# A second block's gates, scans and softplus rounds put in another order

## The chip, the core and the metric

The kernel runs on one core of a Trainium2 chip. The metric is the device time of one execution in microseconds. The kernel before has a median of 1109.62 us over three runs (1109.36 to 1110.53).

## What is computed

The reference runs two transformer blocks on a sequence of 256 tokens of width 1024, all in float32. The first block (an SSD branch and a latent attention, a cross attention, a mixture of 32 experts) is not touched. The second block begins with a mixer, and that is where the change lies:

```python
proj = rmsnorm(h, attn_pre_norm) @ w_in            # 4*512 + 3*512 columns
hq, hf, hi, hg, sq, sk, sv = split(proj)
# HGRN2 on hq, hf, hi: 4 heads of 128
q = silu(hq)
log_f = logaddexp(log(lb), log1p(-lb) + log_sigmoid(hf))
k = -expm1(log_f)                                  # = 1 - f
# o_t = S_t^T q_t, with S_t = diag(f_t) S_{t-1} + k_t v_t^T, v = hi
o_hg = rmsnorm(o, hg_out_norm) * silu(hg)
# stick-breaking attention on sq, sk, sv: 8 heads of 64
z = q k^T / sqrt(64)
a = where(causal, exp(log_sigmoid(z) + rem), 0)    # rem: sum of -softplus(z) over the keys between
o_sb = rmsnorm(a @ v, sb_out_norm)
h = h + rmsnorm(concat(o_hg, o_sb) @ w_out, attn_post_norm)
```

A gated feed forward layer and a gated embedding follow.

## The kernel before

Every large product is made of **units**. A unit is 512 KB of weights: one load on the SP queue into a `raw` buffer (four of them), a cast by ScalarE into `whi` (L237), a subtraction by VectorE into the rest `wlo` (L238), then three matmuls on TensorE for each block of 128 rows (L263 to L265: high by high, and the two mixed ones). Four pairs of whi and wlo exist, and up to three units are split ahead of their use. Units come in a fixed order.

What else an engine does is put between the units by a planner, `schedule`. It takes several streams of `Item`s; an item has a cost, dependencies and for each dependency a latency, which a table (`LATENCY`) can replace by a number for that pair of names ('x#<z#' is any x item behind any z item). It always takes the first stream whose next item is due, and emits the items in that order; each engine then runs its own instructions in the order of emission. `run` emits the units' casts and subtractions ahead of the item that first uses them.

The second block's mixer has five streams: `start` (norms, `prep`), `hg` (HGRN2), `sb` (stick-breaking attention), `nrm` and `main`, which holds the units of w_in, then of w_out. These are the steps that matter here:

- `hqf`: eight chunks of 128 columns of w_in, q's four first, then the gate's four. `ev_hq` empties each chunk's PSUM buffer with a multiplication by the row norm `fr` (L1906) and then applies Silu to q (L1908), or for the gate a Sigmoid (L1911), lb and ol (L1912), max and min (L1913), a second Sigmoid (L1914) and ol (L1915).
- `gates` (item hga): Ln of the gate in place (L1944) and four scans along time (L1947), which read a mask out of the table `c2`; `prep` loads that whole table on POOL's queue (L1876) and sets the two buffers of `ql` and of `kl` to zero with POOL (L1883).
- `level(m)` for m = 128, 64, 32, ... 1 (item lv): differences of the sums, in `E`, on POOL (L1966, L1967, L1975, L1982, L1983), VectorE's t01 and a part of E (L1981, L1984), Exp on ScalarE, and q·E and k·E on VectorE as `ql` (L1992) and `kl` (L1993). `smat(m, t)` (item sm) makes their products on TensorE (L2004) in a PSUM buffer `ch`, of which there are four, and VectorE merges them into `S` (L2010 for the diagonal, a masked copy L2014 for the levels from 64 down).
- `ho`, `hm` and `mt0` close HGRN2: products with v (L2049, L2050), the norm, the gate (hm, L2057), and transposes (L438) whose results are split by ScalarE (mxh, L443) and VectorE (mxl, L444).
- For each of four pairs of heads the stick-breaking stream has `sb_z` (items z: scores L2072 and L2073, a copy L2078, min(z,-z) L2080, Exp and Ln L2081 and L2082, then max and add L2083 and the causal mask L2085), `sb_x` (items x: running sums as matmuls L2095 to L2100, VectorE's addition L2101, Exp L2102) and `sb_pv` (items pv: L2116 to L2118, a copy to `so` by ScalarE L2119).
- `sb_o` (items so) norms the result: two squares with a sum on ScalarE (L410), a power on POOL (L417, L418), a multiplication on VectorE (`hy`, L2038). Then come the transposes mt4 and the units of w_out, the attention's half of whose rows stands first.

Of the kernel before, what the change touches and what calls it, by code (L numbers as in the profile page):

```python
# [112 lines left out]
class K:  # L113
# [260 lines left out]
    def gemm_fm(self, w, c0, nch, kt, xT, evac, name, deps=(), held=None, wide=None):  # L374

        items = []
        hiT, loT = xT
        for i in range(0, nch, 2):  # L380
# [1924 lines left out]
```

## Time and profile before

| | |
|---|---|
| median of three runs | 1109.62 us |
| the profiled execution | 1108.28 us |
| its span, first to last instruction | 1106.5 us |
| TensorE busy | 1049.0 us (95%) |
| VectorE busy | 647.0 us (58%) |
| ScalarE busy | 525.3 us (47%) |
| GpSimd (POOL) busy | 142.2 us (13%) |
| mean granted TensorE clock | 0.979 |

The busy share is a mean over the whole program. The second block's mixer takes some 110 us from about 735 us on, and the views below are of that stretch. The granted clock is the share of full speed that TensorE was given: 1.0 is 2.4 GHz, 0.5 is 1.2 GHz.

### The profile page before, as it was taken

To read this page: it belongs to the slowest core of one execution; us is meant where nothing else is said; L and a number is where in the kernel's file an instruction comes from. 1 tells how busy PE (TensorE), PEld (TensorE's weight loads), DVE (VectorE), ACT (ScalarE), POOL (GpSimd) and SP (SyncE) were. 2 spreads that over 40 slices of the span, in tenths; PEclk is the share of its full clock that TensorE was granted. 3 is DMA by queue.
4 is the path that set the end of the run, shared out by engine and by line. 5 is a ranking of instruction groups with operands and counts; after the bars stand their busy time and mean duration, and the time that the engine had idled before them with its cause. 6 is when DMAs were issued, how large, how long until landed. Compare 5 with 4: busy or idle time off the path is not lost. (4 is left out here: it accounts for less than half of the span.)

```text
span 1106.5 us, 18028 instructions
## 1 busy us (share of the span) xinstructions
PE 1049.0 (95%) x7081; PEld 878.1 (79%) x7081; DVE 647.0 (58%) x1114; ACT 525.3 (47%) x944; POOL 142.2 (13%) x187
## 2 busy tenths in 40 slices
PE   6999999999999899999999897997999999999998
PEld 6999889878887798987766563697888788888876
DVE  4887788766766654545211110278865676667545
...
GB/s 251 193 191 153 130 119 136 133 200 125 137 144 115 315 347 316 160 220 322 421 413 420 412 418 414 312 175 122 188 71 123 134 204 177 190 187 173 221 143 95
DMA packets 135033, 241.29 MB, mean 218 GB/s; under 512 B 6924, under 2 KB 88336, under 8 KB 127776
## 3 DMA queue, kind: packets, MB, share of 16 engines
...
q14 instruction: 32, 0.26, 0.1%
...
## 5 line engine op out<-in xcount | busy, mean ns | idle before, releaser
L238 DVE TENSOR_TENSOR wlo<-raw,whi 128x1024 fp32r<-128x1024 f32 (+1 forms) x240 | 291.5, 1234 | 129.4 <-ACT whi L237 128.5
L237 ACT CAST whi<-raw 128x1024 fp32r<-128x1024 f32 (+1 forms) x240 | 244.9, 1041 | 97.3 <-PE acc L265 51.0
L273 PE MATMUL acc<-ew,whi 128*128 128x512 f32 x352 | 120.5, 394 | 0.8 <-DVE ew L444 0.8
L263 PE MATMUL acc<-uh,whi 128*128 128x256 f32 x384 | 111.2, 290 | 0.0
L264 PE MATMUL acc<-ul,whi 128*128 128x256 f32 x384 | 108.6, 283 | 0.0
L265 PE MATMUL acc<-uh,wlo 128*128 128x256 f32 x384 | 108.5, 283 | 0.0
L276 PE MATMUL acc<-ew,wlo 128*128 128x256 f32 x352 | 92.0, 282 | 0.0
L263 PEld LDWEIGHTS acc<-uh,whi 128*128 128x128 f32 x384 | 73.5, 191 | 0.8 <-issue 0.3
L264 PEld LDWEIGHTS acc<-ul,whi 128*128 128x128 f32 x384 | 73.6, 192 | 0.2
L265 PEld LDWEIGHTS acc<-uh,wlo 128*128 128x128 f32 x384 | 73.5, 191 | 0.0
L273 PEld LDWEIGHTS acc<-ew,whi 128*128 128x128 f32 x352 | 63.1, 188 | 12.6 <-DVE ew L444 1.0
L276 PEld LDWEIGHTS acc<-ew,wlo 128*128 128x128 f32 x352 | 66.1, 188 | 3.8
L1578 PE MATMUL acc<-ew,xe 128*32 128x256 f32 x688 | 57.5, 398 | 7.2 <-DMA ew<-in_w_exp_up_dram 3.7
L1537 PEld LDWEIGHTS acc<-Gr,h 128*128 128x128 f32 x256 | 54.5, 299 | 10.8 <-issue 9.8
L263 PE MATMUL acc<-whi,uh 128*128 128x512 f32 (+1 forms) x160 | 63.0, 394 | 0.0
L264 PE MATMUL acc<-wlo,uh 128*128 128x512 f32 (+1 forms) x160 | 61.5, 384 | 0.6 <-DVE wlo L238 0.6
L265 PE MATMUL acc<-whi,ul 128*128 128x512 f32 (+1 forms) x160 | 61.2, 383 | 0.0
L1537 PE MATMUL acc<-Gr,h 128*128 128x128 f32 x256 | 54.6, 373 | 6.0 <-DVE Gr L1518 6.0
L1578 PEld LDWEIGHTS acc<-ew,xe 128*32 128x32 f32 x688 | 34.5, 114 | 24.9 <-issue 5.9
L265 PE MATMUL acc<-ew,wlo 128*128 128x256 f32 x176 | 50.3, 286 | 0.9 <-DVE wlo L238 0.9
L263 PE MATMUL acc<-ew,whi 128*128 128x256 f32 x176 | 50.4, 286 | 0.8 <-ACT whi L237 0.5
L264 PE MATMUL acc<-ew,whi 128*128 128x256 f32 x176 | 50.3, 286 | 0.2
...
## 6 DMA issues: line engine op xcount, KB each, us to landing
...
```

Source lines behind the costliest of these rows:

```text
L237: self.nc.scalar.copy(hi[:, :m], u.raw[:, :m])
L238: self.nc.vector.tensor_sub(lo[:, :m], u.raw[:, :m], hi[:, :m].bitcast(F32))
L263: mm(out, ah, bh, start=start, stop=False)
L264: mm(out, ah, bl, start=False, stop=False)
L265: mm(out, al, bh, start=False, stop=stop)
L273: mm(out, ah, bw, start=(k == 0), stop=(k == last))
L276: mm(out[:, :T], al, b.hi[:, k, :], start=False, stop=False)
L1537: nc.tensor.matmul(p[:, j * P:(j + 1) * P], x, st["Gr"][:, t, :], start=(part is None and t == 0), stop=(t == 1 and (part is None or j == 3)))
L1578: nc.tensor.matmul(a[j][CAP * i:CAP * i + CAP, :256], xe[:, k, i * CAP:i * CAP + CAP], w, start=(k == 0), stop=(k == 7))
```

## The change

- Two more units are split before the row norm `fr` is computed (`more` twice), and a Sigmoid of one column stands before fr's copy, so that its table is loaded there.
- The gate's four chunks are projected first (`first=4`). Their PSUM buffers are emptied, and Sigmoid, lb and ol, max and min and the second Sigmoid are made over two or four chunks at once, at the fourth chunk; q's Silu is one activation over four chunks, at the last.
- The reset mask has a load of its own, early (`resets`). The table c2 gets 1024 columns of zeros; ql and kl are set to zero by four loads of these columns on POOL's queue, and c2's own load leaves them out.
- The scans wait for the gate's chunks alone, with a latency that puts them behind two splits; Ln goes in two halves. `level` is cut into `expo` (POOL's and VectorE's part of E, emitted two levels ahead) and the rest.
- In the softplus rounds max, add and mask become an item of their own, `sb_e`, between z and x.

In the diff the table's line is cut to the entries that change.

```diff
-C2_M, C2_TGE, C2_RST = 0, 896, 1024
-NCONST2 = 1280
+C2_M, C2_TGE, C2_RST, C2_ZERO = 0, 896, 1024, 1280
+NCONST2 = 2304
...
-LATENCY = {
...
-'sm128<lv128': 1.9,
...
-'hga<hqf.#': 0,
...
-'sm64<lv64': 3.7,
...
+LATENCY = {
...
+'sm128<lv128': 11.5,
...
+'hga<hqf.#': 4.0, 'sm0<hqf.#': 5.5,
...
+'sm64<lv64': 14.0,
...
-def gemm_fm(self, w, c0, nch, kt, xT, evac, name, deps=(), held=None, wide=None):
+def gemm_fm(self, w, c0, nch, kt, xT, evac, name, deps=(), held=None, first=0, wide=None):
...
-            u = self.unit(w, k0, nk, c0 + i * P, 256)
+            u = self.unit(w, k0, nk, c0 + (i + first) % nch * P, 256)
...
+        s = self.sp.tile([P, 4], F32, tag="rstd", name=self.nm("rstd"), bufs=6)
+        nc.scalar.activation(s[:, 0:1], self.half, AF.Sigmoid)
...
-    A["start"] = [Item(hsq(0), name="hs"), Item(more), Item(trans(1), cost=0.9, name="zt", deps=[("hs", 2)]),
+    def resets():
+        A["rst"] = self.sp.tile([P, D], F32, tag="un", name=self.nm("un"), bufs=2)[:, :T]
+        nc.gpsimd.dma_start(A["rst"], I["consts2"][:, C2_RST:C2_RST + T])
+    A["start"] = [Item(resets), Item(hsq(0), name="hs"), Item(more), Item(trans(1), cost=0.9, name="zt", deps=[("hs", 2)]),
...
-                  Item(spread, cost=0.4, name="fr", deps=[("f1", 4)]),
+                  Item(more, deps=[("f1", 3.9)]), Item(more), Item(spread, cost=0.4, name="fr", deps=[("f1", 4)]),
...
-        st["c2"] = pt([P, NCONST2], "c2")
-        nc.gpsimd.dma_start(st["c2"], I["consts2"])
+        st["c2"] = pt([P, C2_ZERO], "c2")
+        nc.gpsimd.dma_start(st["c2"], I["consts2"][:, :C2_ZERO])
...
         for n in ("ql", "kl"):
...
-                nc.gpsimd.memset(st[n, i], 0.0)
+                nc.gpsimd.dma_start(st[n, i].rearrange("p h t -> p (h t)"), I["consts2"][:, C2_ZERO:])
...
     def ev_hq(c, a):
...
-        x = st["q" if c < 4 else "k"][:, c % 4, :]
+        x = st["k" if c < 4 else "q"][:, c % 4, :]
...
-        if c < 4:
-            nc.scalar.activation(x, x, AF.Silu)
-        else:
-            f, lb, ol = st["sig"][:, c - 4, :], self.A["lb"][:, c - 4:c - 3], self.A["ol"][:, c - 4:c - 3]
-            nc.scalar.activation(f, x, AF.Sigmoid)
-            V.tensor_scalar(f, f, ol, lb, op0=ALU.mult, op1=ALU.add)
-            V.tensor_scalar(f, f, 2.0 ** -60, 1.0, op0=ALU.max, op1=ALU.min)
-            nc.scalar.activation(x, x, AF.Sigmoid, scale=-1.0)
-            V.tensor_scalar(x, x, ol, None, op0=ALU.mult)
+        sg, k = st["sig"], st["k"]
+        if c in (1, 3):
+            nc.scalar.activation(sg[:, c - 1:c + 1], k[:, c - 1:c + 1], AF.Sigmoid)
+        if c == 3:
+            for i in range(4):
+                V.tensor_scalar(sg[:, i], sg[:, i], self.A["ol"][:, i:i + 1], self.A["lb"][:, i:i + 1],
+                                op0=ALU.mult, op1=ALU.add)
+                if i % 2:
+                    h = sg[:, i - 1:i + 1]
+                    V.tensor_scalar(h, h, 2.0 ** -60, 1.0, op0=ALU.max, op1=ALU.min)
+            nc.scalar.activation(k, k, AF.Sigmoid, scale=-1.0)
+            for i in range(4):
+                V.tensor_scalar(k[:, i], k[:, i], self.A["ol"][:, i:i + 1], None, op0=ALU.mult)
+        if c == 7:
+            nc.scalar.activation(st["q"], st["q"], AF.Silu)
...
     held = []
-    main = self.gemm_fm(w, 0, 8, 8, U, ev_hq, "hqf", {0: [("hs", 0)], 2: [("zt", 2.5)]}, held)
+    main = self.gemm_fm(w, 0, 8, 8, U, ev_hq, "hqf", {0: [("hs", 0)], 2: [("zt", 2.5)]}, held, first=4)
...
     def gates():
...
-        nc.scalar.activation(sg, sg, AF.Ln)
+        for h in (0, 2):
+            nc.scalar.activation(sg[:, h:h + 2], sg[:, h:h + 2], AF.Ln)
...
-            V.tensor_tensor_scan(b[:, h, :], st["c2"][:, C2_RST:C2_RST + T], sg[:, h, :], 0.0,
+            V.tensor_tensor_scan(b[:, h, :], self.A["rst"], sg[:, h, :], 0.0,
...
-    def level(m):
+    def expo(m):
...
         def fn():
...
-            i = LV.index(m) % 2
-            E = pt([P, 4, T], "E", bufs=2)
-            ql, kl = st["ql", i], st["kl", i]
+            E = st["E", m] = pt([P, 4, T], "E", bufs=2)
...
-                nc.scalar.activation(E, E, AF.Exp)
...
-                v = lambda x: x.rearrange("p h (n s m) -> p h n s m", s=2, m=m)
...
                 if m == 64:
...
-                    nc.scalar.activation(ev[:, :, 0:4:2, :], ev[:, :, 0:4:2, :], AF.Exp)
-                    nc.scalar.activation(ev[:, :, 1:4:2, :], bv[:, :, 1:4:2, :], AF.Exp)
...
-                    nc.scalar.activation(ev[:, :, 2, :], bv[:, :, 2, :], AF.Exp)
-                    nc.scalar.activation(ev[:, :, 3, :], ev[:, :, 3, :], AF.Exp)
-                    nc.scalar.activation(ev[:, :, 0:2, :], ev[:, :, 0:2, :], AF.Exp)
+        return Item(fn, name=f"le{m}")
...
+    def level(m):
...
+        def fn():
+            E, i = st["E", m], LV.index(m) % 2
+            ql, kl = st["ql", i], st["kl", i]
+            bv, ev = (x.rearrange("p h (n m) -> p h n m", m=64) for x in (st["b"], E))
+            if m == 128:
+                nc.scalar.activation(ev[:, :, 2, :], bv[:, :, 2, :], AF.Exp)
+                nc.scalar.activation(ev[:, :, 3, :], ev[:, :, 3, :], AF.Exp)
+                nc.scalar.activation(ev[:, :, 0:2, :], ev[:, :, 0:2, :], AF.Exp)
+            elif m == 64:
+                nc.scalar.activation(ev[:, :, 0:4:2, :], ev[:, :, 0:4:2, :], AF.Exp)
+                nc.scalar.activation(ev[:, :, 1:4:2, :], bv[:, :, 1:4:2, :], AF.Exp)
+            else:
+                nc.scalar.activation(E, E, AF.Exp)
...
-        d = [(f"lv{m}", 8)] if m else [("hga", 6)]
+        d = [(f"lv{m}", 8)] if m else [("hqf.7", 3)]
...
-    hg = [Item(gates, name="hga", deps=[("hqf.7", 1), ("prep", 0)])]
-    hg += [level(128), level(64), smat(0, 0), smat(0, 1)]
+    hg = [Item(gates, name="hga", deps=[("hqf.3", 1), ("prep", 0)])]
+    hg += [expo(128), expo(64), level(128), expo(32), level(64), expo(16), smat(0, 0), smat(0, 1)]
+    hg[3].deps.append(("hqf.7", 0))
...
+        if i + 4 < len(LV):
+            hg.append(expo(LV[i + 4]))
...
-                V.scalar_tensor_tensor(e, z, 0.0, e, op0=ALU.max, op1=ALU.add)
-                for i in (0, 256):
-                    V.tensor_tensor(e[:, :, i:i + P], e[:, :, i:i + P],
-                                    self.c[:, None, C_STR:C_STR + P].to_broadcast([P, 2, P]), op=ALU.mult)
...
+    def sb_e(h):
...
+        def fn():
+            z, e = st["sp", h // 2]
+            V.scalar_tensor_tensor(e, z, 0.0, e, op0=ALU.max, op1=ALU.add)
+            for i in (0, 256):
+                V.tensor_tensor(e[:, :, i:i + P], e[:, :, i:i + P],
+                                self.c[:, None, C_STR:C_STR + P].to_broadcast([P, 2, P]), op=ALU.mult)
+        return Item(fn, name=f"e{h}", deps=[(f"z{h}", 5.0)])
...
     def sb_x(h):
         def fn():
...
-        return Item(fn, cost=1.1, name=f"x{h}", deps=[(f"z{h | 1}", 6)])
+        return Item(fn, cost=1.1, name=f"x{h}", deps=[(f"e{h | 1}", 2.0)])
...
-        sb += [sb_z(h), sb_z(h + 1)] + ([sb_pv(h - 1)] if h else []) + [sb_x(h), sb_x(h + 1)]
+        sb += [sb_z(h), sb_z(h + 1)] + ([sb_pv(h - 1)] if h else []) + [sb_e(h + 1), sb_x(h), sb_x(h + 1)]
...
```

What this does to the engines' order shows at three places. The first is VectorE, from the scans to the first weight split behind the levels 128 and 64 (hb are the scans' results, wlo the rest of a weight split). Before:

```order
L1947 SCALAR_TENSOR_TENSOR hb_8954<-c_1565_8802,hsig_8815 128x256 x4
L1981 TENSOR_TENSOR t_1594_8961<-hb_8954 128x4
L1984 TENSOR_TENSOR E_8960<-hb_8954 128x4x64
L1992 TENSOR_TENSOR ql_8806<-hq_8814,E_8960 128x2x128
L1993 TENSOR_TENSOR kl_8810<-hk_8816,E_8960 128x2x128
L1992 TENSOR_TENSOR ql_8806<-hq_8814,E_8960 128x2x128
L1993 TENSOR_TENSOR kl_8810<-hk_8816,E_8960 128x2x128
L1992 TENSOR_TENSOR ql_8808<-hq_8814,E_8973 128x4x64
L1993 TENSOR_TENSOR kl_8812<-hk_8816,E_8973 128x4x64
L1992 TENSOR_TENSOR ql_8808<-hq_8814,E_8973 128x4x64
L1993 TENSOR_TENSOR kl_8812<-hk_8816,E_8973 128x4x64
L238 TENSOR_TENSOR wlo_8983<-raw_8835,whi_8982 128x1024
```

In the changed kernel, from behind the scans on, up to the split that follows those levels:

```order
L238 TENSOR_TENSOR wlo_8932<-raw_8757,whi_8931 128x1024
L1913 TENSOR_TENSOR hq_8830<-acc_8888,fr 128x256
L1913 TENSOR_TENSOR hq_8830<-acc_8901,fr 128x256
L2014 TENSOR_TENSOR ql_8822<-hq_8830,E_8922 128x2x128
L2015 TENSOR_TENSOR kl_8826<-hk_8832,E_8922 128x2x128
L2014 TENSOR_TENSOR ql_8822<-hq_8830,E_8922 128x2x128
L2015 TENSOR_TENSOR kl_8826<-hk_8832,E_8922 128x2x128
L2014 TENSOR_TENSOR ql_8824<-hq_8830,E_8928 128x4x64
L2015 TENSOR_TENSOR kl_8828<-hk_8832,E_8928 128x4x64
L2014 TENSOR_TENSOR ql_8824<-hq_8830,E_8928 128x4x64
L2015 TENSOR_TENSOR kl_8828<-hk_8832,E_8928 128x4x64
L238 TENSOR_TENSOR wlo_8984<-raw_8763,whi_8983 128x1024
```

The split wlo_8932 and two of q's chunks now stand between scans and levels; two more splits, wlo_8851 and wlo_8883, stand shortly before the scans.

The second is TensorE at the products of the levels 2 and 1 (the last two of the L2004 rows before, and of the L2026 rows after; ch are PSUM buffers). Before:

```order
L2004 MATMUL ch_9473<-ql_8806,kl_8810 128x128 x4
L2004 MATMUL ch_9479<-ql_8806,kl_8810 128x128 x4
L2004 MATMUL ch_9485<-ql_8808,kl_8812 128x128 x4
L2004 MATMUL ch_9491<-ql_8808,kl_8812 128x128 x4
L263 MATMUL acc_9349<-whi_9343,ew_8519 128x512
```

and in the changed kernel:

```order
L2026 MATMUL ch_9486<-ql_8822,kl_8826 128x128 x4
L2026 MATMUL ch_9492<-ql_8822,kl_8826 128x128 x4
L2026 MATMUL ch_9498<-ql_8824,kl_8828 128x128 x4
L2026 MATMUL ch_9504<-ql_8824,kl_8828 128x128 x4
L2147 MATMUL ch_9511<-sv_9477,sbz_9331 128x64
L2148 MATMUL ch_9511<-sv_9477,sbz_9331 128x64
L2149 MATMUL ch_9511<-sv_9477,sbz_9331 128x64
```

Before, the unit whi_9343 stood between these products and the first pv (L2116, behind that unit); now the pv (L2147) follows at once, and a unit comes behind it.

The third is TensorE from the last pv on. Before, the last rows of the pv and the beginning of the unit behind it:

```order
L2116 MATMUL ch_9764<-sv_9509,sbz_9628 128x64
L2117 MATMUL ch_9764<-sv_9509,sbz_9628 128x64
L2118 MATMUL ch_9764<-sv_9509,sbz_9628 128x64
L263 MATMUL acc_9750<-whi_9641,ew_8518 128x512
L264 MATMUL acc_9750<-wlo_9642,ew_8518 128x512
L265 MATMUL acc_9750<-whi_9641,ew_8518 128x512
```

and the end of the second unit behind it, the attention's transposes (of hy_9778) and the unit behind these:

```order
L264 MATMUL acc_9757<-wlo_9660,ew_8519 128x512
L265 MATMUL acc_9757<-whi_9659,ew_8519 128x512
L438 MATMUL ch_9823<-ident,hy_9778 128x128 x4
L438 MATMUL ch_9830<-ident,hy_9778 128x128 x4
L263 MATMUL acc_9750<-whi_9744,ew_8519 128x512
L264 MATMUL acc_9750<-wlo_9745,ew_8519 128x512
L265 MATMUL acc_9750<-whi_9744,ew_8519 128x512
```

In the changed kernel (hy_9692 are HGRN2's, hy_9831 the attention's rows, acc_9875 belongs to w_out):

```order
L2147 MATMUL ch_9816<-sv_9477,sbz_9662 128x64
L2148 MATMUL ch_9816<-sv_9477,sbz_9662 128x64
L2149 MATMUL ch_9816<-sv_9477,sbz_9662 128x64
L438 MATMUL ch_9841<-ident,hy_9692 128x128 x4
L438 MATMUL ch_9848<-ident,hy_9692 128x128 x4
L438 MATMUL ch_9855<-ident,hy_9831 128x128 x4
L438 MATMUL ch_9862<-ident,hy_9831 128x128 x4
L263 MATMUL acc_9875<-whi_9741,mxh_9672 128x512
L264 MATMUL acc_9875<-wlo_9742,mxh_9672 128x512
L265 MATMUL acc_9875<-whi_9741,mxl_9673 128x512
```

Before, two units stood between pv and transposes, and a third between these and w_out; now none does, and HGRN2's transposes stand there as well.

## Rows read from the trace of the kernel before

**Rows 1.** The page, part 1: busy time, share and instructions of each engine.

```profile
PE 1049.0 (95%) x7081; PEld 878.1 (79%) x7081; DVE 647.0 (58%) x1114; ACT 525.3 (47%) x944; POOL 142.2 (13%) x187
```

**Rows 2.** Stretches: us, busy us (count) of PE, PEld, DVE, ACT, POOL, granted clock, DMA.

```profile
757.00:771.00 14.00, 8.75 (x45) 8.30 (x46) 12.40 (x19) 8.59 (x12) 9.05 (x8) 0.63 0.22 67
795.00:804.00 9.00, 7.04 (x47) 6.23 (x46) 8.97 (x18) 4.50 (x5) 0.01 (x1) 0.81 0.75 277
804.00:863.00 59.00, 58.80 (x355) 50.64 (x354) 34.79 (x45) 42.30 (x62) 3.54 (x8) 1.00 0.35 107
```

**Rows 3.** TensorE's waits, 720 to 850 us: total, times, longest.

```profile
PE ch L2004 <- DVE kl L1993: 5.7, 2, 4.2
PE ch L2095 <- DVE S L2014: 2.0, 1, 2.0
PE acc L265 <- DVE wlo L238: 0.9, 2, 0.8
...
PE ch L2116 <- DVE S L2014: 0.2, 1, 0.2
```

**Rows 4.** Single microseconds, columns as in rows 2.

```profile
758.00:759.00 1.00, 0.00 (x0) 0.00 (x0) 0.54 (x3) 0.81 (x2) 0.68 (x1) 0.89 0.00 0
769.00:770.00 1.00, 1.00 (x10) 1.00 (x10) 1.00 (x1) 0.71 (x1) 0.26 (x1) 0.99 0.65 148
```

**Rows 5.** TensorE's timeline: start, us, instruction, idle before.

```profile
754.61 1.95 PE L2004 MATMUL ch<-hq,hk 128*128 128x128 f32 x16
760.79 2.31 PE L2004 MATMUL ch<-ql,kl 128*128 128x128 f32 x8 [4.23 <-DVE kl L1993]
764.56 3.78 PE L2004 MATMUL ch<-ql,kl 128*128 128x128 f32 x16 [1.46 <-DVE kl L1993]
```

**Rows 6.** VectorE's groups, 735 to 772 us: busy, mean ns, idle before.

```profile
L238 DVE TENSOR_TENSOR wlo<-raw,whi 128x1024 fp32r<-128x1024 f32 x8 | 10.5, 1356 | 1.8 <-ACT whi L237 1.8
L1992 DVE TENSOR_TENSOR ql<-hq,E 128x256 f32<-128x256 f32 x5 | 3.3, 659 | 1.2 <-ACT E L1978 0.6 <-ACT E L1987 0.6
L1993 DVE TENSOR_TENSOR kl<-hk,E 128x256 f32<-128x256 f32 x5 | 3.0, 591 | 0.4 <-ACT E L1988 0.4
L1947 DVE TENSOR_TENSOR_SCAN hb<-c,hsig 128x256 f32<-128x256 f32 x4 | 2.4, 673 | 1.8 <-ACT hsig L1944 1.8
L1915 DVE TENSOR_SCALAR hk<-hk,lb 128x256 f32<-128x256 f32 x4 | 2.2, 541 | 0.0
L1913 DVE TENSOR_SCALAR hsig<-hsig 128x256 f32<-128x256 f32 x4 | 1.9, 471 | 0.1
L1912 DVE TENSOR_SCALAR hsig<-hsig,lb 128x256 f32<-128x256 f32 x4 | 1.7, 433 | 1.9 <-ACT hsig L1911 1.9
```

**Rows 7.** VectorE's timeline, 735 to 750 us.

```profile
735.85 1.42 DVE L1906 TENSOR_TENSOR hq<-acc,fr 128x256 f32<-128x256 f32 x4 [1.80 <-ACT fr L1802]
...
743.53 1.00 DVE L1913 TENSOR_SCALAR hsig<-hsig 128x256 f32<-128x256 f32 x1
```

**Rows 8.** DMA issues, 735 to 760 us: KB each, median us to landing.

```profile
c<-in_consts_dram POOLq DMA_DIRECT2D x1, 640.0 KB, 7.1
```

**Rows 9.** VectorE's timeline, a softplus round.

```profile
794.04 0.96 DVE L2083 SCALAR_TENSOR_TENSOR sbe<-sbz,sbe 128x768 f32<-128x768 f32 x1 [3.07 <-ACT sbe L2082]
```

**Rows 10.** ScalarE's timeline, the same round.

```profile
791.87 1.28 ACT L2082 ACT_TABLE_LOAD   x1
```

**Rows 11.** ScalarE's timeline, the join of the streams.

```profile
844.13 0.37 ACT L2119 COPY so<-ch 128x256 f32<-128x256 f32 x1 [2.38 <-PE ch L2118]
...
850.21 1.07 ACT L443 CAST mxh<-ch 128x512 fp32r<-128x512 f32 x2 [2.19 <-PE ch L438]
```

**Rows 12.** VectorE's timeline, the join.

```profile
847.67 0.75 DVE L2038 SCALAR_TENSOR_TENSOR hy<-so,rpow,ghs 128x512 f32<-128x512 f32 x1 [0.72 <-POOL rpow L418]
...
850.83 1.29 DVE L444 TENSOR_TENSOR mxl<-ch,mxh 128x512 fp32r<-128x512 f32 x2
```

**Rows 13.** TensorE's timeline, the join.

```profile
849.58 1.03 PE L438 MATMUL ch<-ident,hy 128*128 128x128 f32 x8
```

More of the change, by code (lines that the diff above doesn't have):

```diff
@@ new lines @@
+LATENCY = {'-<cols': 0, 'g2.fin<g2.nrm': 1.9, 'g1.fin<g1.nrm': 2.6, 'u31<p11': 3.8, '-<h50': 1.3, 'g2.y1<g2.d#': 7.0, 'p11<y1r.1': 4.3, '-<mt#.#': 5.8, 'g1.y3<z#.#': 13.9, '-<u31': 9.0, 'q#.#<q#.#': 2.3, 'xs#.#<qx.#': 10.1, 'xv#<vx.#': 0.3, 'y2r.1<y2.1': 0.2, 'sm4<lv4': 9.6, 'g3.y1<g3.d#': 6.1, 'g2.y1<g2.xt#': 16.5, 'g0.y0<z#.#': 13.4, 'g1.sil<z#.#': 0, 'pv#<x#': 4.8, '-<u30': 1.4, 'g3.y2<g3.xt#': 4.4, 'g0.y1<g0.xt#': 15.2, 'xt#.#<xs#.#': 3.7, 'g3.y0<z#.#': 7.8, 'g0.y2<z#.#': 0.9, 'g2.nrm<g2.y3': 5.2, 'g1.d#<g1.cb': 2.9, 'p21<y2r.1': 0, 'ho#<hv.#': 3.6, 'p10<y1r.0': 0.3, 'g0.y1<g0.d#': 9.8, 'g2.cb<acum': 3.3, '-<tr#': 5.0, '-<pv#': 2.1, 'sm128<lv128': 11.5, 'h51<p21': 3.0, 'g1.y0<g1.d#': 0, 'g0.y0<g0.xt#': 10.3, 'g3.y1<g3.xt#': 11.5, 'g2.y0<g2.xt#': 10.5, '-<nx#': 2.2, 'g1.y1<z#.#': 17.4, 'y2r.0<y2.0': 0.5, 'g3.y0<g3.d#': 6.6, 'acum<dt': 5.6, '-<wxo.#': 2.5, 'g3.sil<z#.#': 2.7, 'pv#<sv.#': 0, 'xs#.#<kx.#': 17.4, 'pv#<v#.#': 3.3, 'g0.sil<z#.#': 14.0, 'hga<prep': 12.4, '-<g1.y3': 3.1, 'sm16<lv16': 8.1, 'k#.#<k#.#': 0.7, 'sm32<lv32': 11.8, 'g3.y2<g3.d#': 8.6, 'g1.y0<g1.xt#': 0.5, 'sm0<hga': 6.0, 'g2.y0<z#.#': 4.6, 'g0.d#<g0.d#': 11.9, 'g3.d#<g3.cb': 0.6, 'v#.#<k#.#': 0, 'g0.y2<g0.xt#': 9.0, 'h50<p20': 8.1, 'bcs<bc.#': 9.5, 'hga<hqf.#': 4.0, 'sm0<hqf.#': 5.5, '-<g0.y3': 0.4, 'g0.y2<g0.d#': 13.1, 'g1.y3<g1.d#': 4.2, 'sm8<lv8': 8.5, 'g3.y2<z#.#': 3.4, 'nxb0<nxa0': 17.1, 'g3.cb<bcs': 4.7, 'nxa0<wo.#': 2.7, 'kpb<acum': 6.4, 'g3.y0<g3.xt#': 11.0, 'u31<p1b1': 0.4, 'g2.d#<g2.cb': 0, 'g0.fin<g0.nrm': 1.6, 'g1.y3<g1.xt#': 14.8, 'g1.y0<g0.fin': 5.6, 'z#<sqk.#': 8.4, 'g3.xt#<g3.sil': 1.8, 'g2.y3<g2.xt#': 7.6, 'g0.y3<z#.#': 11.5, 'g2.y1<z#.#': 3.8, 'g2.y2<g2.xt#': 4.1, 'g1.y2<g1.xt#': 11.2, 'g1.cb<bcs': 4.8, 'g0.xt#<g0.sil': 3.3, 'g2.sil<z#.#': 15.0, 't#<s#': 0, '-<g0.fin': 15.9, 'g0.cb<bcs': 3.1, 'sm2<lv2': 6.8, 'p1b1<p11': 5.4, 'g1.y2<z#.#': 5.6, '-<pT': 5.7, 'p1b0<p10': 3.2, '-<wxo.a': 11.5, 'g1.y1<g1.d#': 16.1, 'u30<p1b0': 3.7, 'g0.d#<g0.cb': 2.2, 'nxa1<wo.#': 3.3, '-<m#': 12.1, '-<h51': 2.4, 'pv#<t#': 5.4, '-<g1.fin': 0.3, 'g1.cb<acum': 15.0, 'mla#<kpe': 0.8, 'g0.y3<g0.xt#': 10.8, 'g3.y1<z#.#': 8.6, 'g3.fin<g3.nrm': 2.5, 'dtb<sm.#': 2.6, 'g0.y1<z#.#': 10.4, 'g1.xt#<g1.sil': 8.9, 'g3.nrm<g3.y3': 1.0, 'g3.y3<g3.xt#': 8.0, 'nx0<nxb0': 2.3, '-<nx1': 7.5, 'g1.y1<g1.xt#': 4.3, '-<vx.#': 2.7, 'p1b0<p1a0': 5.0, 'g0.sil<x#.#': 4.2, 'm#<pt': 13.7, 'g3.sil<x#.#': 2.3, 'g2.y0<g2.d#': 8.8, 'g2.y0<g1.fin': 8.8, '-<prep#': 1.1, 'sm64<lv64': 14.0, 'kpe<kpb': 3.5, 'g0.y3<g0.d#': 13.7, 'y1r.1<y1.1': 10.8, '-<xv#': 11.4, 'g2.y2<z#.#': 1.9, 'nxb1<nxa1': 0, 'nx1<nxb1': 0.5, 'g3.y3<z#.#': 0.5, 's#<q#.#': 0, 'p1a1<p11': 1.8, 'mla#<qn': 2.6, 'pm<g3.fin': 0.6, 'g0.y0<g0.d#': 10.8, 's#<k#.#': 1.5, 'g2.y2<g2.d#': 9.3, 'g1.y2<g1.d#': 1.9, 'g2.y3<z#.#': 1.0, 'g1.d#<g1.d#': 0.8, 'g0.d#<g0.cb0': 0, '!main': 5, 'g1.nrm<g1.y3': 5.2, 'g0.nrm<g0.y3': 3.1, 'g0.d#<g0.d#1': 0, 'cols<small': 26.8, 'g0.cb<acum': 0.6, 'g1.sil<x#.#': 6.9, 'g1.y0<z#.#': 7.9, 'g3.y3<g3.d#': 6.8, 'g2.xt#<g2.sil': 3.7, 'g0.d#<g0.d#0': 3.5, 'g3.cb<acum': 12.2, 'g2.d#<g2.cb0': 2.5, 'g3.y0<g2.fin': 4.4, 'g2.sil<x#.#': 13.5, 'g2.cb<bcs': 14.0, 'qnb0<qna1': 3.2, 'kpb<kpa': 3.9, 'v#.#<v#.#': 0, 'g2.y3<g2.d#': 7.3, 'q#.#<v#.#': 0.5, '-<qnb0': 10.2, 'g1.d#<g1.d#0': 14.2, 'g1.d#<g1.cb0': 4.9, 'dt<dtb': 13.3, 'g3.d#<g3.d#0': 0, 'g2.d#<g2.d#0': 3.2, 'g2.d#<g2.d#1': 0, 'g3.d#<g3.cb0': 0.4, 'tr#<ymo.#': 12.8, 'g3.d#<g3.d#1': 0, 'xv#<xt#.#': 1.3, 'hqf.#<prep#': 10.2, '-<n#': 8.8, '-<z#': 12.0, '-<rl#': 0, '-<u#': 1.7, 'z#<n#': 6.6, 'hqf.#<fr': 12.0, 'ho#<hg.#': 1.1, 'g1.d#<g1.d#1': 0, 'sm1<lv1': 4.8, 'p1a0<p10': 0, 'fr<f#': 11.9, 'p20<y2r.0': 2.5, 'ho#<sm1': 3.6, 'p1b1<p1a1': 5.0, '!DC': 0, '!CB': 0, '!CA': 0, '!DA': 0, 'hm0<hg.0': 1.0, 'hm1<hg.1': 1.0, 'mt0.0<hm0': 0.6, 'mt0.1<hm1': 4.1, 'mt4.0<so0': 5.0, 'mt4.1<so1': 5.0, '-<mt4.1': 2.5, 'hm0<hg.#': 2.3, 'mt4.1<so#': 5.6, 'hm1<hg.#': 2.0, '-<mt0.1': 10.7, 'x#<z#': 5.1}
```

1 line of the change is left out of this document (removed).

## The prediction

> **What bounds the kernel now.** I read the page first: TensorE is busy 1049.0 us of the 1106.5 us span [rows 1], so an edit counts only where it changes a moment at which TensorE stands still or runs at a lowered clock. The sums of stretches then show where that is around the change [rows 2]. In 757 to 771 us TensorE works 8.75 of 14 us at a mean granted clock of 0.63; in 795 to 804 us 7.04 of 9 us at 0.81; from 804 to 863 us it loses 0.2 us. After that the order is the old one. TensorE's waits name the causes [rows 3]: 5.7 us in two waits for VectorE's kl (L1993), 2.0 us before L2095 for the masked copy that empties a PSUM buffer (L2014), 0.2 us before L2116, and 0.9 us for a weight split, all else being small. The timeline of the first hole shows what stands behind the waits [rows 5]: 16 products of L2004 take 1.95 us, but after 4.23 us of idling 8 take 2.31 us, and the next 16 take 3.78 us. Those are the two clock levels (2.4 and 1.2 GHz): the granted clock falls in the slice 758 to 759 us, some 2 us after TensorE ran dry, and is back only between 769 and 770 us [rows 4], 4.4 to 5.4 us after the products at 764.56 us [rows 5]. Half speed over 4.4 us of work costs 2.2 us. [...]
>
> The sum is made against the profiled execution, 1108.3 us, which lies 1.3 us below the median of the runs, 1109.6.
>
> **Part A, the gates and scans.** Before, VectorE goes from the scans through all ql/kl, and TensorE waits for these. Now three weight splits stand among them, so that TensorE has units to work on, and what it waits for is the split behind ql/kl 64 (wlo_8984). VectorE's work from its first multiplication to that split is, by its rows [rows 6]: 4 gate multiplications 1.4 [rows 7], 4 lb/ol 1.7, 2 max/min (as wide as two old ones each; one took 1.00 us [rows 7]) 2.0, 4 multiplications of k 2.2, 4 splits of 1.3 together 5.2, 4 multiplications of q 1.4 like those, the scans 2.4, t01 and E about 0.6 (as less than two multiplications), 4 ql and 4 kl at 0.66 and 0.59 together 5.0. Sum 21.9 us. Its start was 735.85 us [rows 7] and moves to about 736.5, as the two earlier splits and casts stand ahead of it. With no wait it would end at 758.4. The scans waited 1.8 us for Ln [rows 6]; two splits now fill part of that, and I add 0.8: 759.2. TensorE reaches its first 16 products over a microsecond earlier than before, as the 0.9 us wait for a split [rows 3] goes, finishes them by 755 and idles about 4 us. From 759.2 it needs 8 and 16 products at 0.12 us, 2.9 us, to stand where before it stood at 767.99 with half a microsecond of low clock left, i.e. at 768.5; with the clock's 2.2 us that is 764.3. **Gain 4.2 us.** Ends: 1 us (the whole 1.8 us wait remains and one more split is late) and 8 us (hole under 2 us, no fall of the clock).
>
> The memsets become four fills of 512 KB on POOL's queue. The nearest row is the load of c2 on that queue: 640 KB land 7.1 us after issue [rows 8]. Issued where the memsets stood, about 742.5 us, they land by some 750 to 752 us; ql and kl are first written after 752. So I take 0, with ends of 0 and 2 us late. The row that bears on fills beside VectorE is the old max/min: one took 1.00 us beside a memset [rows 7], while the mean of the four is 0.47 [rows 6]; VectorE and POOL delay each other here. The Trainium skill ("SBUF — State Buffer", Who interferes with whom) states this as a lock of a port pair and speaks against the change: POOL-queue DMAs stall when VectorE holds the pair, since POOL writes their descriptors. No run here shows that case; by it the fills would come late, and the time would go the way of the last rival. Reset mask, dummy Sigmoid, Ln in halves and the one Silu lie beside TensorE's units; without that cover the one table load more would cost 1.28 us [rows 10].
>
> **Part B, the softplus rounds.** Splitting max/add from Exp and Ln fills VectorE's idle of 3.07 us in each round with splits [rows 9]. That in itself helps nobody on TensorE after 804 us, where nothing is lost. What counts is the new order. x0 and x1 still follow the products of levels 8 and 4 directly, and the masked copies still stand behind a split: 2.0 us of wait [rows 3] and 1.7 of clock (9 us at 0.81 [rows 2]) as before, no change. But the first pv now follows the products of levels 2 and 1 directly; before, a whole unit stood between, and 0.2 us of wait was left [rows 3]. A unit takes 2.7 us (two fill the 5.45 us from the last pv to 849.58 [rows 11, 13]). Now these are uncovered: 2.9 us with the rest, and 2.2 of clock: +5.1 us. The unit follows later and is not lost work, but it covers nothing there. The x's of the last rounds follow with one unit less ahead of them; I add 0.8 us. **Loss 5.9 us**; ends: 0, if Exp, casts and splits come as early as the planner's table assumes, and 7.4, with the whole of a second clock fall.
>
> **Part C, the join.** Before, the last pv ends at 844.13 us, when ACT copies its output [rows 11]; two units follow on TensorE until the transposes at 849.58 us [rows 13], and these hide the out norm entirely. Now the planner has put both hg transposes, both sb transposes and then w_out behind the last pv with no unit between. The chain there, by its rows: from the copy to the end of the second hy 847.67+0.75-844.13 = 4.3 us [rows 11, 12]; the product with the gate (hm1), now queued behind both hy's on VectorE and as wide as hy, 0.75; 12 transposes 1.5 (8 took 1.03 [rows 13]); the last cast of mxh 0.54 [rows 11]; the last mxl 0.65 [rows 12]. That is 7.7 us, of which TensorE works about 2.1 (16 transposes): idle 5.7, and 2.2 for the clock. **Loss 7.9 us**, ends 5.7 and 9.
>
> **Sum.** -4.2 + 5.9 + 7.9 = +9.6: 1117.9 on the profiled execution, **1119.2 on the median's footing; I say 1119.0.**
>
> **Rivals.** About 0.2% (2.2 us) is what a measurement of this kernel tells from no change.
> 1. *The rounds stay hidden* (B at its end of 0): the waits in that stretch are only 2.2 us now, and VectorE gets 3.07 us of idling per round back. Against it: the unit is gone from between. 1109.6-4.2+7.9 = 1113.3.
> 2. *The join is covered*, because TensorE reaches pv7 late and hg's part was ready, and the chain is mostly overlapped: speaks against it that hy depends on pv7 itself [rows 11, 12]. 1109.6-4.2+5.9 = 1111.3, within 0.2%.
> 3. *Faster: VectorE's relief decides.* VectorE is the releaser in each long wait of the list [rows 3]. If the idle of 3.07 us in each round [rows 9] carries the splits, pv1 doesn't wait and the masked copy before x0 comes 2 us earlier (B -3.7); and if ql/kl, no longer beside POOL's E, take 0.4 us instead of 0.6, the split after them comes at about 757, the hole stays under 2 us and the clock holds (A -8). It decides from a split before 757 us on. 1109.6-8-3.7+7.9 = 1105.8.
> 4. *The fills or E come late*: A's gain goes and 2 us come on top: 1109.6+2+5.9+7.9 = 1125, with some of the waits overlapping about 1123.5.
>
> **How the numbers follow.** Forecast 0.52: its two losses rest on the order of the instructions and on chains of measured rows. Rival 1 0.14, since B is the sum with the least evidence in rows. Rival 2 0.09. Rival 3 0.20, because VectorE's waits carry the present losses and its idle is real; the join speaks against it. Rival 4 0.05. Slower by over 0.2%: 0.52+0.14+0.05 = 0.71; within 0.2%: 0.09; faster: 0.20. The forecast's own range goes from 1113.5 (B at 1, C at 5.7) to 1124 (A at 1, rest as it is, B 7.4). The whole range leaves out rival 3 and starts at 1108, which takes in rival 2 with a larger gain of A; its upper end is 1124.
>
> **What would show it.** In the new profile the waits of TensorE should name the wlo split (L238) once with some 4 us in the stretch about 755 to 760, in place of two for kl; a wait of about 3 us before the first pv (L2147), on a masked copy; and at about 845 to 852 a hole of 5 to 6 us before the first matmuls of w_out, waiting for hy, mxh and mxl, each followed by a stretch at half clock. VectorE's idle before L2114 should be gone. The prediction is wrong if TensorE is busy throughout from the last pv to w_out, or if the granted clock stays at 1.0 from 755 to 770.

## The result and the profile after

The changed kernel takes 1118.46 us in the median of four runs (1117.27 to 1120.61), against 1109.49 us of the kernel before: a ratio of 1.0082, with a 95% interval of 1.007 to 1.0094, or 9.0 us more. The prediction said 1119.0. The profiled execution took 1117.27 us; it and the profiled ones of several runs below lie under the medians of their kernels (u_nomore's the most, by 2.8 us), so the waits of a trace need not add up to a difference of medians.

The page says nearly the same as before [rows 1]: the span is 1115.5 us instead of 1106.5, but TensorE has only 1.8 us more of busy time, so the rest is standing still:

```profile
PE 1050.8 (94%) x7081; PEld 879.9 (79%) x7081; DVE 648.0 (58%) x1112; ACT 525.3 (47%) x939; POOL 141.2 (13%) x188
```

TensorE's waits from 720 to 880 us (total, times, longest) name other causes than before [rows 3]. The two waits for kl are gone, 5.7 us; in their place stand a weight split in the first hole, the masked copy ahead of the first pv (L2147), and hy ahead of the transposes (L438):

```profile
PE ch L438 <- DVE hy L2082: 4.6, 1, 4.6
PE acc L265 <- DVE wlo L238: 3.3, 2, 2.9
PE ch L2147 <- DVE S L2036: 3.0, 1, 3.0
PE ch L2126 <- DVE S L2036: 1.5, 1, 1.5
PE acc L263 <- ACT whi L237: 1.0, 1, 1.0
...
PE ch L2127 <- DVE sbe L2116: 0.9, 1, 0.9
```

The stretches answer to [rows 2] (us, busy us and count of PE, PEld, DVE, ACT and POOL, granted clock, DMA share, GB/s; the instruction that makes fr on TensorE, ahead of the changed stretch, stands 1.4 us later in this execution, at 736.2 against 734.8). The first hole is smaller and its clock better, 0.76 against 0.63; before x0 the clock now holds, 1.00 against 0.81; but from 804 us on, where 0.2 us were lost, TensorE now stands still for 3.9 of 47 us and then for 4.6 of 19:

```profile
757.00:771.00 14.00, 10.16 (x64) 9.76 (x63) 13.15 (x20) 7.16 (x10) 6.25 (x4) 0.76 0.54 166
795.00:804.00 9.00, 7.38 (x57) 6.69 (x57) 8.96 (x18) 3.77 (x4) 0.00 (x0) 1.00 0.82 295
804.00:851.00 47.00, 43.07 (x264) 36.94 (x264) 24.35 (x34) 31.50 (x45) 1.50 (x4) 0.96 0.26 79
851.00:870.00 19.00, 14.44 (x71) 11.90 (x70) 9.82 (x12) 10.63 (x16) 2.04 (x4) 0.91 0.29 85
```

Single microseconds of the same view show the granted clock on its way from 1.0 (2.4 GHz) to 0.5 (1.2 GHz) in three places, the first hole, behind the first pv and in the join, and where it is back after the last:

```profile
760.00:761.00 1.00, 0.00 (x0) 0.00 (x0) 1.00 (x3) 1.00 (x2) 0.21 (x2) 0.79 0.00 0
815.00:816.00 1.00, 1.00 (x4) 0.84 (x3) 0.97 (x2) 1.00 (x2) 0.00 (x0) 0.60 0.29 109
859.00:860.00 1.00, 0.00 (x0) 0.00 (x0) 1.00 (x2) 0.00 (x0) 0.00 (x0) 0.78 0.00 0
863.00:864.00 1.00, 1.00 (x5) 0.57 (x5) 0.84 (x2) 0.92 (x2) 0.00 (x0) 1.00 0.00 0
```

### The profile page after: what moved, and what is told of

The parts are those of the page before. It is cut to its first block, busy times and chain, and to the rows that moved or that the text cites. A ratio compares the mean times of both kernels' runs of the same rounds, so it can differ in the third digit from the quotient of the medians.

```text
span 1115.5 us, 18034 instructions
## 1 busy us (share of the span) xinstructions
PE 1050.8 (94%) x7081; PEld 879.9 (79%) x7081; DVE 648.0 (58%) x1112; ACT 525.3 (47%) x939; POOL 141.2 (13%) x188
```

## The experiments

In the order of the argument, not all in the order in which they ran. A ratio is to the kernel before, with its 95% interval.

### The gates' part alone (unsplit)

Max, add and mask go back into z; everything else of the change stays.

```diff
                 nc.scalar.activation(e, e, AF.Ln, bias=1.0)
+                V.scalar_tensor_tensor(e, z, 0.0, e, op0=ALU.max, op1=ALU.add)
+                for i in (0, 256):
+                    V.tensor_tensor(e[:, :, i:i + P], e[:, :, i:i + P], ...
...
-    return Item(fn, cost=1.1, name=f"x{h}", deps=[(f"e{h | 1}", 2.0)])
+    return Item(fn, cost=1.1, name=f"x{h}", deps=[(f"z{h | 1}", 6)])
...
-    sb += ... + [sb_e(h + 1), sb_x(h), sb_x(h + 1)]
+    sb += ... + [sb_x(h), sb_x(h + 1)]
```

> The changed kernel with max, add and mask put back into z, so that only the gates' part of the change is left; TensorE's order is that of x0. Theory: 1106 to 1108, as the gates alone gain 3 us; x0 differs from it by less than 1.5 us. Rival (the gates' part gains nothing, the early fr and fills cost as much): 1109.5 or more.

Measured 1106.33 us, ratio 0.9963 (0.9951 to 0.9976): 4.1 us faster than before by the ratio, 3.5 by the medians. The gates' part gains what part A said (4.2 us), with an interval of 2.7 to 5.4 us, and the separated max and add cost the other way: 1118.46 - 1106.33 = 12.1 us.

### The order kept, max and add still apart (x0)

```diff
-'x#<z#': 5.1}
+'x#<z#': 5.1, 'x#<e#': 0}
```

> The changed kernel with one number changed: the planner's latency of x behind e is 0 instead of 2.0, so that the extra item costs no planning step; TensorE's order then has a unit between the products of levels 2 and 1 and the first pv again, and two units between the last pv and the transposes. Everything else of the change stays. Theory (the order of pv and units makes the loss, the gates gain about 3 us): 1118.5 less 4 for the first pv and 6 for the join, 1107 to 1109. Rival (the separated max and add, the fills or the gates make the loss): 1115 or more.

Measured 1123.56 us, ratio 1.0126 (1.0107 to 1.0144). The theory fell, and the rival that blames the separated max and add holds. TensorE's order is the same as in unsplit, and yet it takes 17.2 us more. The waits name one cause, max, add and mask themselves (L2116 is the mask):

```profile
PE ch L2127 <- DVE sbe L2116: 12.0, 4, 5.6
```

VectorE's timeline of one round in x0 shows why (start, us, instruction, idle before):

```profile
824.75 0.96 DVE L2105 SCALAR_TENSOR_TENSOR sbe<-sbz 128x768 f32<-128x768 f32 x1 [1.91 <-ACT sbz L2103]
829.72 2.36 DVE L238 TENSOR_TENSOR wlo<-raw,whi 128x1024 fp32r<-128x1024 f32 x2 [4.01 <-ACT whi L237]
832.00 0.95 DVE L2114 SCALAR_TENSOR_TENSOR sbe<-sbz,sbe 128x768 f32<-128x768 f32 x1
```

and the same place in unsplit:

```profile
827.94 0.96 DVE L2105 SCALAR_TENSOR_TENSOR sbe<-sbz 128x768 f32<-128x768 f32 x1 [1.34 <-ACT sbz L2103]
831.97 0.96 DVE L2108 SCALAR_TENSOR_TENSOR sbe<-sbz,sbe 128x768 f32<-128x768 f32 x1 [3.07 <-ACT sbe L2107]
```

In unsplit, max and add follow min directly; VectorE idles 3.07 us until Ln is done and starts them at once. In x0 the planner emits them as an item of their own, behind two splits. The casts of these stand behind Ln on ScalarE, so VectorE idles still longer, 4.01 us, then makes two splits and only then max and add: 6.3 us after min's end instead of 3.1. On TensorE nothing covers this, and the clock falls with the four waits: from 785 to 852 us TensorE's mean granted clock is 0.85 there.

```profile
785.00:852.00 67.00, 54.63 (x302) 47.46 (x301) 33.98 (x53) 36.74 (x48) 6.38 (x8) 0.85 0.26 87
```

### Exp and Ln moved with them (mid05c)

If the splits ahead of max and add are the cause, one split between z and Exp, where ScalarE and VectorE wait anyway, should cost nothing.

```diff
-                nc.scalar.activation(e, e, AF.Exp)
-                nc.scalar.activation(e, e, AF.Ln, bias=1.0)
...
     def sb_e(h):
...
+            nc.scalar.activation(e, e, AF.Exp)
+            nc.scalar.activation(e, e, AF.Ln, bias=1.0)
             V.scalar_tensor_tensor(e, z, 0.0, e, op0=ALU.max, op1=ALU.add)
...
-    sb += ... + ([sb_pv(h - 1)] if h else []) + [sb_e(h + 1), sb_x(h), sb_x(h + 1)]
+    sb += ... + [sb_e(h + 1)] + ([sb_pv(h - 1)] if h else []) + [sb_x(h), sb_x(h + 1)]
...
+'e#<z#': 0.1, 'x#<e#': 2.0
```

> The changed kernel with Exp and Ln moved into the separate item with max, add and mask, which is emitted directly behind the next unit's beginning, so that one cast and one subtraction stand between z's min and Exp, and not two behind Ln ahead of max and add; TensorE's order is that of unsplit and x0. Theory (what costs is how many splits stand ahead of max and add on VectorE, and their casts behind Ln): most of x0's loss of 17 us goes, 1105 to 1111. Rival (any separate item is late, whatever stands ahead): 1115 or more.

Measured 1106.40 us, ratio 0.9970 (0.9961 to 0.9980). All 17 us of x0 are gone, with the same order on TensorE. A round on VectorE:

```profile
825.71 0.96 DVE L2105 SCALAR_TENSOR_TENSOR sbe<-sbz 128x768 f32<-128x768 f32 x1 [1.34 <-ACT sbz L2103]
826.66 1.22 DVE L238 TENSOR_TENSOR wlo<-raw,whi 128x1024 fp32r<-128x1024 f32 x1
829.74 0.96 DVE L2114 SCALAR_TENSOR_TENSOR sbe<-sbz,sbe 128x768 f32<-128x768 f32 x1 [1.86 <-ACT sbe L2113]
```

One split of 1.22 us now lies in the idle time, of which 1.86 us is left, and max and add start 3.1 us after min's end, as in unsplit. So a separate item need not cost anything. That the number of splits ahead of max and add decides is read from these timelines; no run changes that number alone. mid05c is no faster than unsplit: no wait of TensorE in the rounds names one of these splits.

### Only the split of max and add, in the kernel before (only_e)

The kernel before gets `sb_e` and the change's latencies, and nothing else of the change.

```diff
+    def sb_e(h):
...
-    sb += ... + [sb_x(h), sb_x(h + 1)]
+    sb += ... + [sb_e(h + 1), sb_x(h), sb_x(h + 1)]
```

> The kernel before with only max, add and mask made an item of their own, with the change's latencies. TensorE's order has a unit ahead of the first pv, but half of the transposes and w_out directly behind the last pv. Theory: the join alone is uncovered, 1109.5 and 5 to 7, so 1114 to 1117. Rival (filling VectorE's idle of 3 us in each round is worth something by itself, and the loss comes with the gates): 1108 to 1111.

Measured 1128.35 us, ratio 1.0162 (1.0144 to 1.0179), far above the theory's 1114 to 1117, which counted the join alone. The waits add a round's max and add (L2091 is the mask) and sv:

```profile
PE ch L2102 <- DVE sbe L2091: 4.2, 1, 4.2
PE ch L438 <- DVE hy L2038: 3.4, 2, 3.0
PE ch L2122 <- ACT sv L1921: 3.1, 1, 3.1
```

So the part costs more without the gates' part than with it. In its trace sv stands on ScalarE behind the round's Exp, Ln and a cast: z's copy begins at 817.79 us and sv at 823.13. How the loss divides was not followed up.

### The join alone (u_join)

unsplit with the last pv held back until w_in's units are through, so that TensorE goes from it into the four transposes and w_out, as in the changed kernel.

```diff
-    deps=[(f"x{h}", 4.5), ("sv.1", 1.5)]
+    deps=[(f"x{h}", 4.5), ("sv.1", 1.5)] + ([("hg.1", 0)] if h == 7 else [])
```

> The gates' part alone (as in the run unsplit, 1106.3), with the last pv held back until the last unit of w_in is done, so that TensorE goes from the last pv directly into all four transposes and w_out, as in the changed kernel; nothing else moves. Theory (the join costs by itself what the prediction's chain says): a wait of 4 to 5 us for hy before the second transposes, then a low clock, 1106.3 and 6 to 8: 1112 to 1114.5. Rival (the loss at the join was a consequence of the late max and add): below 1108.5.

Measured 1112.68 us, ratio 1.0022 (1.001 to 1.0034): 6.3 us more than unsplit. The wait is the changed kernel's own, to the tenth:

```profile
PE ch L438 <- DVE hy L2082: 4.6, 1, 4.6
```

### The first pv alone (pvlate)

The changed kernel with the first pv held behind the products of level 1, so that a unit stands between them again.

```diff
-    deps=[(f"x{h}", 4.5), ("sv.1", 1.5)]
+    deps=[(f"x{h}", 4.5), ("sv.1", 1.5)] + ([("sm1.1", 2.5)] if h == 1 else [])
```

> The changed kernel with the first pv held 2.5 us behind the products of level 1, so that a unit stands between them again; the join is still uncovered (the last pv is followed by two transposes and w_out, with HGRN2's two transposes ahead of it). Theory (the first pv's wait of 3.0 us and the low clock behind it are local to that place): 1118.5 less 4 to 5.5, 1113 to 1114.5. Rival (the unit is missed elsewhere, since the stream has no spare ones): 1116.5 or more.

Measured 1112.06 us, ratio 1.0023 (1.0011 to 1.0034): 6.4 us less than the changed kernel. The planner moved the join a little too, so not all of it belongs to the first pv; its own wait falls from 3.0 to 0.3 us, hy's from 4.6 to 3.4:

```profile
PE ch L438 <- DVE hy L2063: 3.4, 2, 3.0
...
PE ch L2147 <- DVE S L2036: 0.3, 1, 0.3
```

### The fills (u_memset)

unsplit with POOL's memsets in place of the four loads.

```diff
-    nc.gpsimd.dma_start(st[n, i].rearrange("p h t -> p (h t)"), I["consts2"][:, C2_ZERO:])
+    nc.gpsimd.memset(st[n, i], 0.0)
```

> The gates' part alone, with ql and kl set to zero by POOL's memsets as in the kernel before instead of by loads. Theory (the loads are hidden and cost nothing, the memsets stand 4 us on POOL and delay E of level 128 or VectorE's max and min a little): 1106 to 1109. Rival (2 MB of zeros delay the weight loads, or come late): faster than 1105.

Measured 1106.51 us, ratio 0.9966 (0.9955 to 0.9977), as unsplit. The loads cost nothing and gain nothing that these runs can tell.

### What in the gates' part gains (u_nomore, b_more)

unsplit without the two splits ahead of fr:

```diff
-    Item(more, deps=[("f1", 3.9)]), Item(more), Item(spread, ...
+    Item(spread, ...
```

> The gates' part alone without the two splits that the change puts ahead of the row norm fr. Theory (these two cover the first units behind fr; without them the small waits of 0.9 us for wlo and 0.5 us for whi that the kernel before had there return, and VectorE starts about as much earlier): 1106 to 1108.5. Rival (they are what makes the gates' gain): 1109.5 or more.

Measured 1111.45 us, ratio 1.0006 (0.9991 to 1.0022): the whole gain is gone, and the rival holds. TensorE's waits and VectorE's timeline of u_nomore:

```profile
PE acc L265 <- DVE wlo L238: 5.6, 2, 3.1
...
PE acc L263 <- ACT whi L237: 1.8, 1, 1.8
```

```profile
735.22 1.42 DVE L1913 TENSOR_TENSOR hk<-acc,fr 128x256 f32<-128x256 f32 x4 [1.75 <-ACT fr L1805]
...
741.73 3.48 DVE L238 TENSOR_TENSOR wlo<-raw,whi 128x1024 fp32r<-128x1024 f32 x3
```

The gate's batch keeps VectorE from 735 to 742 us, ahead of three splits, and TensorE, which has no split unit left, waits 1.8 us for whi and 3.1 for wlo. The two early splits are the batch's cover. The other half of the question is the kernel before with these two splits and nothing else:

```diff
-    Item(spread, cost=0.4, name="fr", deps=[("f1", 4)])
+    Item(more, deps=[("f1", 3.9)]), Item(more), Item(spread, cost=0.4, name="fr", deps=[("f1", 4)])
```

> The kernel before with nothing changed but the two more splits ahead of the row norm fr; the order of q's and the gate's chunks, scans, levels and rounds stays. Theory (the two splits cover the gates' batch on VectorE, and are worth little without it: only the small waits of 0.9 us for wlo and 0.5 us for whi go, while the first hole, behind scans and ql and kl, stays): 1108 to 1110.5. Rival (the two splits alone make the gain of the gates' part): 1107 or less.

Measured 1109.50 us, ratio 1.0004 (0.9989 to 1.0019): no change that the interval shows, and TensorE still waits 5.9 us for kl. So neither the two splits nor the rest of the gates' part gains by itself; together they do. That it is the batch which the splits cover is read from the timeline above.

### The first hole (x0_lv1, u_lv1, m_l64_20)

Level 128 held 1 us behind q's last chunk, in x0 and in unsplit:

```diff
-    hg[3].deps.append(("hqf.7", 0))
+    hg[3].deps.append(("hqf.7", 1.0))
```

> x0 with level 128 held 1 us behind the last chunk of q, so that one more unit's cast and subtraction stand before the Exps and ql/kl. Theory (in the first hole TensorE waits for a split that stands behind ql and kl): the wait of 2.9 us for wlo goes, and with it the low clock, 3 to 5 us less than x0; but the first pv again follows the products directly, 4 more: 1106 to 1109. Rival (the hole only moves to the products, which then wait for ql and kl): no gain, 1110 to 1113.

> The gates' part alone, with level 128 held 1 us behind q's last chunk, so that one more unit's split stands before ql and kl, and the first pv follows the products of levels 2 and 1 directly. Theory (the first hole's 3.2 us wait for the split shrinks to a later wait of the kind x0_lv1 showed, 2.9 us for sq, and the first pv waits about 2 us): between -2 and +2 of unsplit, 1104.5 to 1108. Rival (the hole closes): 1103 or less.

Measured 1121.65 us (1.0113, 1.0093 to 1.0133) and 1109.08 us (0.9989, 0.9978 to 1.0). The first expectation stood on x0 being fast, which it isn't; beside x0 it is 1.9 us less, which the intervals do not tell apart. Beside unsplit the same edit is 2.7 us more, above the 1104.5 to 1108 that were expected. The hole moved: in u_lv1 a split now stands ahead of ql and kl, and TensorE waits 2.9 us for a multiplication of sq behind them, and 3.1 us before the first pv.

```profile
PE ch L2141 <- DVE S L2036: 3.1, 1, 3.1
PE acc L263 <- DVE sq L1942: 2.9, 1, 2.9
```

mid05c with level 64 behind the first products instead:

```diff
-    hg += [expo(128), expo(64), level(128), expo(32), level(64), expo(16), smat(0, 0), smat(0, 1)]
+    lv64 = level(64)
+    lv64.deps.append(("sm0.1", 2.0))
+    hg += [expo(128), expo(64), level(128), smat(0, 0), smat(0, 1), expo(32), lv64, expo(16)]
```

> mid05c (1106.4) with level 64 put behind the first products and 2 us later, so that the first hole's split stands behind level 128's ql and kl alone and not behind level 64's. Theory (TensorE waits there for VectorE to get through ql and kl): the wait of 2.9 us for wlo falls to about 1 and the clock doesn't fall for so long, 3 to 5 us less, 1101.5 to 1104, if the softplus rounds, whose order moves too, wait no more than before. Rival (level 64 comes late and the rounds pay for it): 1106 or more.

Measured 1105.01 us, ratio 0.9955 (0.9943 to 0.9966), the fastest of all: 5.0 us under the kernel before. In the hole the theory holds, the clock stays at 1.00:

```profile
751.00:774.00 23.00, 21.09 (x171) 20.52 (x171) 19.60 (x30) 14.15 (x17) 12.37 (x9) 1.00 0.71 231
```

But of the expected 3 to 5 us under mid05c only 1.4 are measured. The softplus rounds, whose order the planner moved too, wait 3.0 us for the mask, where mid05c waited 2.4, and 1.2 for the masked copy, where it had no such wait; that is 1.8 us of what is missing:

```profile
PE ch L2129 <- DVE sbe L2118: 3.0, 2, 2.4
...
PE ch L2128 <- DVE S L2036: 1.2, 1, 1.2
```

## Why the prediction was right

The sum was +9.6 us and the measurement is +9.0, and the terms hold one by one: -4.2 against -4.1 (unsplit), +7.9 against +6.3 (u_join beside unsplit), +5.9 against 12.1 - 6.3 = 5.8 for the rest of the softplus part. (These add up to 8.0 and not 9.0, as the first goes by the ratio and the others by medians of different sessions.) So the three terms do not make up for each other's errors. But by the intervals each of these measured terms is uncertain by 1.4 to 2 us, so agreement to a tenth is luck; and inside the terms steps were wrong, some of which make up for each other. The lower end of the forecast's own range is added up wrongly: B at 1 and C at 5.7 give 1109.6 - 4.2 + 1 + 5.7 = 1112.1, not 1113.5.

**Part A: the size and the place are right, the chain is not, and the size is luck in part.** TensorE idles where it was said to, for the split behind ql and kl: 1.0 us for its whi and 2.9 for its wlo, where about 4 were forecast, and the clock falls behind it. But the step "With no wait it would end at 758.4", to which 0.8 us was added for Ln, was wrong. VectorE and ScalarE in the changed kernel:

```profile
756.10 0.43 DVE L2014 TENSOR_TENSOR ql<-hq,E 128x256 f32<-128x256 f32 x1 [3.22 <-ACT E L2004]
...
757.95 1.26 DVE L2015 TENSOR_TENSOR kl<-hk,E 128x256 f32<-128x256 f32 x1
759.13 1.29 DVE L2014 TENSOR_TENSOR ql<-hq,E 128x256 f32<-128x256 f32 x1
...
760.68 3.19 DVE L238 TENSOR_TENSOR wlo<-raw,whi 128x1024 fp32r<-128x1024 f32 x2
```

```profile
752.91 1.06 ACT L1928 ACTIVATE hq<-hq 128x1024 f32<-128x1024 f32 x1 [5.49 <-DVE hq L1913]
753.99 1.28 ACT L2003 ACT_TABLE_LOAD   x1
```

VectorE idles 3.22 us before the first ql, for Exp (L2004). ScalarE makes Silu once for four chunks of q only after the last of them is there, then loads the table for Exp (1.28 us), then makes the Exps; the prediction put that Silu among what lies "beside TensorE's units". The eight ql and kl together took what was forecast, 5.1 us against 5.0: six took 0.41 to 0.43 us each and not 0.66 and 0.59, but the two beside POOL's work took 1.26 and 1.29. So the split came later than the forecast 759.2 us. What saved the sum is that TensorE, too, ran dry later than the forecast 755:

```profile
755.65 1.95 PE L2026 MATMUL ch<-hq,hk 128*128 128x128 f32 x16
...
761.95 0.58 PE L265 MATMUL acc<-ew,wlo 128*128 128x256 f32 x1 [2.88 <-DVE wlo L238]
```

It was through with its first products at 757.6 us, behind a wait of 0.9 us for VectorE's hq that the prediction did not have and with fr 1.4 us later in this execution; it went on at 761.95. Both ends of the hole moved by some 2.7 us, and its length stayed. Nor is the gain the hole's alone: u_nomore and b_more show that batch and early splits go together, where the prediction counted the splits as 0.9 us.

**The fills** cost 0, as taken (u_memset). They land 6.9 and 9.3 us after issue, in the median, where the nearest row, the load of c2, had 7.1 [rows 8]:

```profile
ql<-in_consts_dram POOLq DMA_DIRECT2D x2, 512.0 KB, 6.9
kl<-in_consts_dram POOLq DMA_DIRECT2D x2, 512.0 KB, 9.3
```

That is just in time: no wait for a fill shows in the changed kernel, but in unsplit VectorE waits 0.42 us for one of kl's fills and 0.29 for the other.

```profile
756.24 0.42 DVE L2015 TENSOR_TENSOR kl<-hk,E 128x256 f32<-128x256 f32 x1 [0.42 <-DMA kl<-in_consts_dram]
```

The rule of the Trainium skill on DMAs of the POOL queue ("SBUF — State Buffer", Who interferes with whom), by which the fills would have come late, spoke against the change. Here they cost nothing that a run can tell, so the last rival did not come.

**Part B: the sum is right, a mechanism was missed.** The first pv waits 3.0 us (2.9 forecast) and the clock falls behind it; the late x waits 0.9 (0.8 forecast). The masked copies that the first pv waits for stand behind a split, and VectorE idles 4.00 us for the cast of this split, which ScalarE makes only behind the round's Ln:

```profile
811.12 1.22 DVE L238 TENSOR_TENSOR wlo<-raw,whi 128x1024 fp32r<-128x1024 f32 x1 [4.00 <-ACT whi L237]
812.26 2.55 DVE L2036 COPY_PREDICATED S<-c,ch 128x512 f32<-128x512 int32 x4
```

The step "x0 and x1 ... as before, no change" was too dear: the wait is 1.5 us instead of 2.0, and the clock does not fall, about 2 us less in all. By these rows B is some 4 us (3.0, some 2 for the clock and 0.9, less 2), where the runs leave 5.8; where the rest lies is not shown. Missed was what the new order is made of. The prediction said that separating max and add fills VectorE's idle with splits and that this "helps nobody"; x0 shows that it harms: the idle grows from 3.07 to 4.01 us, and max and add then stand behind those splits. In the changed kernel the planner knows of a longer way from z to x, 5.0 and 2.0 instead of 5.1, and puts TensorE's x and pv later. That hides the delay on VectorE and uses up the units that had covered the first pv and the join. The order that the prediction rested on was the way in which the late max and add were paid for: 12.1 us, less than the 17.2 of x0, which kept the old order.

**Part C: right mechanism, 1.6 us too much.** The chain from the last pv to the second transposes runs as forecast:

```profile
857.28 0.75 DVE L2063 SCALAR_TENSOR_TENSOR hy<-so,rpow,ghs 128x512 f32<-128x512 f32 x1 [2.37 <-POOL rpow L418]
...
859.42 0.68 DVE L2082 TENSOR_TENSOR hy<-hy,hg 128x512 f32<-128x512 f32 x1
...
863.69 0.69 DVE L444 TENSOR_TENSOR mxl<-ch,mxh 128x512 fp32r<-128x512 f32 x1 [0.16 <-ACT mxh L443]
```

```profile
860.25 2.79 PE L438 MATMUL ch<-ident,hy 128*128 128x128 f32 x12 [4.56 <-DVE hy L2082]
862.86 0.55 PE L263 MATMUL acc<-whi,mxh 128*128 128x512 f32 x1
```

TensorE idles 4.56 us before the second transposes; the 12 of them take 2.79 us at the low clock instead of some 1.5 (8 took 1.03 [rows 13]): 4.6 + 1.3 = 5.9 of the 6.3 us. Two steps were too dear. The idle of 5.7 us counted the last mxl, but w_out's first matmul starts at 862.86, before the last mxl begins at 863.69. And the clock's price of 2.2 us was taken from 4.4 us of work at half speed; here the clock is back in the slice 863 to 864, after less than 3 us of work. Nor does every such wait cost it: in b_more TensorE waits 2.4 us for a wlo, and the granted clock is 1.00 from 747 to 757 us, the stretch around it.

Rival 1 fell: the rounds did not stay hidden. Rival 2 fell with u_join. Rival 3 fell, as the separated max and add gave VectorE no relief that reaches TensorE; with them undone, though, the kernel is faster by the gates' part.
